# A layer of state-space mixer, cross-attention and 32 experts on one core: two experts' tokens gathered together, and a front in another order

## The chip, the cores and the metric

The kernel is one program on one core of a Trainium2 chip, all in float32. The metric is device time in microseconds; the kernel before has 1097.64 us as the median of three runs (1095.42 to 1098.23). The core's engines are TensorE (PE, with its weight loads shown apart as PEld), VectorE (DVE), ScalarE (ACT), GpSimd (POOL) and SyncE (SP, which here only issues transfers). Data come from HBM through 16 DMA engines into SBUF; TensorE writes its products into eight PSUM banks. A float32 product shows as two MATMUL records in the trace.

## The reference, cut to what matters

256 tokens of 1024 values go through one layer:

```
u, xq = split(x @ w_in, [768])
y_mix = s5(u)                     # 48 groups: y = sum_k C A^k B u, then gelu, then a gated linear unit
y_mem = softmax(xq k^T / 8) v     # k = mem @ mem_w_k, v = mem @ mem_w_v, 4 heads
h     = layer_norm(2**0.25 * x + concat(y_mix, y_mem) @ w_out)
gates, experts = top 4 of softmax(h @ router_w + router_b)
for each expert e of 32:          # its own tokens only
    gu = h[tokens] @ w_gu[e] + b_gu[e]               # 1024 x 2048
    a  = min(gu0, 7) * sigmoid(1.702 * min(gu0, 7)) * (clip(gu1, -7, 7) + 1)
    out[tokens] += gate * (a @ w_down[e] + b_down[e])  # 1024 x 1024
return layer_norm(2**0.25 * h + out)
```

Every expert's weights are read once: 8 MB and 4 MB, 32 times.

## The kernel before, in words

SBUF holds one big tile of 22 slots of 8 KB per partition (1 MB each). The table `slot_of` (L85 to L92) says which names share a slot one after the other, such as "win_2 tz1 gb". The experts' weights stream through a ring (L99) of ten blocks of two slots: one block is 2 MB, an expert takes six of them (four for gate and up, two for down), and a block's transfer is issued by SP, in program order, once the last reader of whatever stood in its two slots is done. All transfers have eight lanes: the ninth waits for the first to land. So the first ten blocks depend on when the front of the kernel lets go of its slots, and the later ones on TensorE's progress in the expert loop.

**The front.** L180 to L228 issue the loads: the rows of the state matrix (`araw`, `ldt`) on ACT's queue, all others on SP's. TensorE turns `araw` into the bank `pp`; VectorE copies it to `par` (L239) and from there computes for the 48 groups the powers of the state matrix, a long chain of small operations, and then the tables `m1p0..2` and `m20..2` (`power`, L468 to L479: two products of 128x2048 and one sum, the second product in a scratch slot `ptmp0` or `ptmp1`; the sum is on GpSimd unless another engine is named). Beside that TensorE transposes x, projects it (`ups`, `qps`), and from `m1p` makes the kernel rows `kb`, which ACT copies to `kr`. VectorE adds the skip weights `dsk` to `kr` (L562), and TensorE turns the result (`kc`, L613 to L619) into the Toeplitz tiles `tz0..2`; these are set to zero first (L546 to L548) and completed by `shifted(b)` (L621), five copies on ACT each. Then come the scores, `m1tp`, `sip`, `stp`, `vmp`, the two passes of `yb` (Toeplitz, L757; with the states `xs`, L818), the softmax's scaling of `prob` by ACT (L736 to L739) and its transposes (`pTp`), the gated linear unit (`zp`), the output projection `yp` (L924 to L945), and the norm.

**The output projection.** Four banks (two token halves i, two column halves hf) sum over eight rows q of `w_out`. The first two are done early (`out_mem`). Of the others, q from 2 to QO - 1 go round the four banks in turn; then each bank in turn gets the rest and is added and measured by VectorE at once. QO is 6. Token half 0 can be normed when its two banks are done.

**The expert loop** (L1252 to L1301). One expert in TensorE's order: `up` (`gu_e`, 64 records, four blocks), the sum of the pair before (`cb_e`, after even experts) or the transposed gates (`ogp_e`, after odd ones), `gather` for the next expert (`xgp_e`: eight column blocks of h times a 128x64 one-hot, two token halves, 32 records), the transposed activations (`atp_e`), the next expert's bias products (`gu_e<-bgu`), and `down` (`dn_e`, 32 records, two blocks). VectorE and ACT do the activation (`act`, L1071) beside it. At expert 22 a block leaves the ring and is used for the rows of the end (`late` with the experts' biases, `rows2` with the last norm's rows); expert 26 transposes the gates and adds the biases (`combine(..., late)`), expert 28 spreads the norm's rows (`spread_gb2`, `bc_e`). The end (`finish`, L1207) norms the sum and writes it.

The order of each queue is pinned to program order in the front (`pin`, L116) for PE, DVE, ACT and SP; GpSimd's and the loop's DVE and ACT instructions are placed by a scheduler.

```
        up(ps, xg, lambda kt: gu[kt], ...)
        ...
            xg = gather_of(e + 1)
            slot_gates_of(e + 1)
        ...
        at = act_t(f"e{e}", a)
        if e + 1 < NE:
            ps = up_bias(f"e{e + 1}", sel_of(e + 1))
        down(f"e{e}", at, ...)
```

## Time and profile before

| what | value |
|---|---|
| median of three runs | 1097.64 us |
| the profiled execution | 1097.22 us, of which 1095.4 us are the span that the profile shows |
| PE busy | 1057.1 us (97%) |
| DVE, ACT, POOL busy | 283.1, 152.6, 44.9 us |
| moved by DMA | 424.69 MB |

The share of busy time is a mean over two very different stages: a front of some 164 us, in which a chain runs through VectorE, ACT and TensorE, and the expert loop, in which TensorE and the DMA engines are both busy almost always. The rows of each stage are therefore read by themselves: the profile's strips by slices and stretches tell what the DMA engines did, the chain of waits tells which of the two ended last, and the timelines tell what the front waited for.

### The profile page before, as it was taken

Reading aid. Unit: us, or ns where it says so; the run is one execution under the profiler, and the core shown is the slowest. Engines: PE = TensorE matmul, PEld = TensorE weight load, DVE = VectorE, ACT = ScalarE, POOL = GpSimd, SP = SyncE. Lnnn points to the kernel's source line nnn. Section 1 sums busy time; section 2 is a strip of 40 time slices with the busy share of each in tenths; the row PEclk is TensorE's granted clock in tenths of the full one; section 3 lists DMA queues with packets and bytes.
Section 4 is the critical chain, followed back from the end, with each engine's and each line's share of the span. In section 5 each row is a group of like instructions: output and inputs, shape, how many; then the busy total and the mean of one; then the engine's idle time right before and its main releaser. Section 6 shows DMA issues by size and latency. Waiting matters only on the chain.

```text
span 1095.4 us, 13424 instructions
## 1 busy us (share of the span) xinstructions
PE 1057.1 (97%) x5781; PEld 503.2 (46%) x5781; DVE 283.1 (26%) x632; ACT 152.6 (14%) x287; POOL 44.9 (4%) x57
## 2 busy tenths in 40 slices
PE   8988999999999999999999999999899999999994
PEld 7875664444444444444444443434343444444331
DVE  6895052121212121212121212111121212121204
ACT  2475111100000000000001010000000000010002
POOL 1700030000000000000000000000000000000001
PEclk9999999999999999999999999999999999999998
DMA  9838968999999999999999999999999999999991
GB/s 301 128 113 284 425 249 346 427 427 426 427 425 428 428 424 428 428 425 427 427 426 427 427 427 427 427 427 425 415 426 427 427 427 428 425 427 427 426 393 56
DMA packets 43813, 424.69 MB, mean 388 GB/s; under 512 B 11311, under 2 KB 14275, under 8 KB 19173
## 3 DMA queue, kind: packets, MB, share of 16 engines
q1 hardware_dynamic: 43268, 423.23, 94.0%
q8 instruction: 47, 0.77, 0.3%
q10 hardware_dynamic: 480, 0.55, 0.1%
q14 instruction: 18, 0.14, 0.0%
HBM read 421.93 MB, written 1.84 MB: 387 GB/s over the span
## 4 chain that ended last, share of the span: by engine, by line
PE 68%; DMA 16%; DVE 1%; ACT 0%; issue 0%; ACTq 0%; POOL 0%; DVEq 0%; SPq 0%
PE gu_e L142 34%; PE dn_e L142 17%; DMA big<-in_exp_w_gu_dram 12%; PE xgp_e L142 9%; PE cb_e L142 5%; DMA big<-in_exp_w_down_dram 4%; PE atp_e L145 1%; DVE big L135 0%; PE accp L142 0%; PE ogp_e L145 0%; PE lgp L142 0%; PE bc_e L142 0%; DVE st L135 0%; PE busy L142 0%; PE hTp L145 0%
## 5 line engine op out<-in xcount | busy, mean ns | idle before, releaser
L142 PE MATMUL gu_e<-big,xg_e 128*64 128x512 f32 x2048 | 448.1, 593 | 12.1 <-DMA big<-in_exp_w_gu_dram 11.2
L142 PEld LDWEIGHTS gu_e<-big,xg_e 128*64 128x64 f32 x2048 | 145.6, 137 | 308.6 <-issue 281.3
L142 PE MATMUL dn_e<-big,xl_te 128*64 128x512 f32 x1024 | 226.8, 595 | 0.7 <-ACT xl_te L135 0.7
L142 PEld LDWEIGHTS dn_e<-big,xl_te 128*64 128x64 f32 x1024 | 70.7, 137 | 154.0 <-issue 127.9
L142 PEld LDWEIGHTS xgp_e<-oh_e,big 128*128 128x128 f32 x1024 | 124.4, 196 | 7.2 <-issue 4.0
L1074 DVE TENSOR_SCALAR xl_e<-gu_e 128x512 f32<-128x512 f32 x32 | 22.1, 692 | 405.9 <-PE gu_e L142 405.9
L142 PE MATMUL xgp_e<-oh_e,big 128*128 128x64 f32 x1024 | 124.4, 280 | 0.0
L1103 DVE COPY y_e<-dn_e 64x512 f32<-64x512 f32 x32 | 21.9, 684 | 257.6 <-PE dn_e L142 257.6
L135 ACT ACTIVATE sg_e<-xl_e 128x512 f32<-128x512 f32 x32 | 20.1, 630 | 383.5 <-DVE xl_e L1074 383.5
L142 PE MATMUL cb_e<-y_e,ogT_e 128*128 128x512 f32 x120 | 55.8, 604 | 0.0
L135 ACT COPY y_e<-dn_e 64x512 f32<-64x512 f32 x32 | 18.6, 582 | 259.1 <-DVE y_e L1103 251.9
L135 ACT COPY xg_e<-xgp_e 128x512 f32<-128x512 f32 x32 | 18.7, 585 | 161.7 <-PE xgp_e L142 161.7
L148 DVE TENSOR_TENSOR big<-big,cb_e 128x512 f32<-128x512 f32 x56 | 36.1, 681 | 6.1 <-PE cb_e L142 6.1
L142 PEld LDWEIGHTS cb_e<-y_e,ogT_e 128*128 128x128 f32 x120 | 21.6, 189 | 32.6 <-issue 29.4
L142 PE MATMUL gu_e<-bgu,ident 32*64 32x512 f32 x256 | 34.8, 612 | 0.0
L135 DVE TENSOR_TENSOR big<-big 128x768 f32<-128x768 f32 (+10 forms) x37 | 27.9, 763 | 15.4 <-ACT big L135 14.3
L151 DVE TENSOR_SCALAR oh_e<-iota,rk 128x64 f32<-128x64 f32 x62 | 12.9, 252 | 71.3 <-PE xgp_e L142 71.3
L142 PE MATMUL yp<-big 128*128 128x512 f32 x64 | 28.2, 595 | 0.0
L135 DVE TENSOR_TENSOR big<-big,tab 128x2048 f32<-128x2048 f32 x12 | 26.6, 2280 | 3.5 <-POOL big L148 3.3
L148 POOL TENSOR_TENSOR big<-big 128x512 f32<-128x512 f32 (+1 forms) x10 | 26.0, 2617 | 14.6 <-DVE big L135 13.8
L1182 POOL MEMSET big<- 128x1280 f32 (+1 forms) x2 | 2.1, 1058 | 576.1 <-PE gu_e L142 576.1
L1076 DVE TENSOR_SCALAR xr_e<-gu_e 128x512 f32<-128x512 f32 x32 | 22.1, 692 | 3.1 <-PE gu_e L142 0.2
(260 smaller groups left out, 567.1 us busy)
## 6 DMA issues: line engine op xcount, KB each, us to landing
big<-in_exp_w_gu_dram SPq DMA_DIRECT2D x128, 2048.0 KB, 31.1
big<-in_exp_w_down_dram SPq DMA_DIRECT2D x63, 2048.0 KB, 32.2
big<-in_l_w_in_dram SPq DMA_DIRECT2D x8, 512.0 KB, 8.5
big<-in_w_out_dram SPq DMA_DIRECT2D x3, 1024.0 KB, 8.1
big<-in_x_dram SPq DMA_DIRECT2D x4, 512.0 KB
big<-in_l_s_w_glu_dram SPq DMA_DIRECT2D x2, 768.0 KB
big<-in_mem_dram SPq DMA_DIRECT2D x1, 1024.0 KB
big<-in_mem_w_k_dram SPq DMA_DIRECT2D x1, 1024.0 KB
```

What stands on the lines that cost most here:

```text
L135: return lambda *a, **k: pin(f(*a, **k))
L142: pin(PE.matmul(o, lhsT, rhs, start=start, stop=stop, skip_group_check=shared))
L145: pin(PE.transpose(o, in_, ident if idn is None else idn))
L148: return (eng or V).tensor_tensor(out=o, in0=x0, in1=x1, op=op)
L151: return (eng or V).tensor_scalar(out=o, in0=x0, scalar1=s1, scalar2=s2, op0=op0, op1=op1)
L1074: V.tensor_scalar(out=xl_, in0=ps[0], scalar1=7.0, scalar2=None, op0=ALU.min)
L1076: V.tensor_scalar(out=xr, in0=ps[1], scalar1=7.0, scalar2=-7.0, op0=ALU.min, op1=ALU.max)
L1103: eng(y[:, 512 * dh : 512 * dh + 512], ps[dh][64 * dh : 64 * dh + 64, :])
L1182: G.memset(t[:, 0:width], 0.0)
```

## The change

It has four parts.

1. **The loop.** `gather` takes a list of ranks: after an odd expert it gathers the tokens of the next two at once (a 128x128 one-hot, two banks), and after an even one nothing. The first two experts are still gathered singly. The sigmoid is written over the bank of its input (`sg = ps[0]`) instead of a tile of SBUF. 
2. **The rows of the end.** A block leaves the ring at expert 18 instead of 22, the biases are added at expert 20 instead of 26, the norm's rows are spread at expert 24 instead of 28.
3. **The first loads.** `araw` goes first on SP's queue, one half of x on ACT's; `w_in` comes in 5 transfers instead of 8, with the state's input rows between them; `dsk` in one instead of four.
4. **The order of the front's sums.** The sum of `m1p2` goes from GpSimd to VectorE, that of `m21` from VectorE to GpSimd; the zeroing of `tz0` and `tz1` goes ahead of the sums of `m20` and `m21`; `shifted(2)` goes ahead of the second half of `vmp`; QO is 4. For the earlier zeroing, `tz0..2`, `wo3` and `wgl0` change slots, and the ring's order follows.

```diff
-        "ptmp0 wsc", "ptmp1 gt", "m20", "m21", "m22", "u_sb", "cab s_in tw yg", "memT xs", "bbt wo3", "bab att",
...
+        "ptmp0 wsc", "ptmp1 gt", "m20", "m21", "m22", "u_sb", "cab s_in tw yg", "memT xs", "bbt tz0", "bab att",
...
-    ring = [2 * k + n for k in (0, 1, 2, 3, 4, 5, 6, 7, 9, 8) for n in range(0, 2, ROWS)]
+    ring = [2 * k + n for k in (0, 1, 2, 3, 4, 6, 8, 7, 9, 5) for n in range(0, 2, ROWS)]
...
+    SP.dma_start(araw[:, 0, :], a_re)
     S.dma_start(ldt, log_dt.rearrange("(g o) -> g o", o=1))
-    S.dma_start(araw[:, 0, :], a_re)
-    S.dma_start(araw[:, 1, :], a_im)
-    for i in range(2):
-        SP.dma_start(x_sb[:, i, :], x[0, i * P : (i + 1) * P, :])
+    SP.dma_start(araw[:, 1, :], a_im)
+    S.dma_start(x_sb[:, 0, :], x[0, 0:P, :])
+    SP.dma_start(x_sb[:, 1, :], x[0, P : 2 * P, :])
...
-        for k in range(2):
-            kt = 2 * k2 + k
-            SP.dma_start(t[:, k, :], w_in[kt * P : (kt + 1) * P, :])
-            win.append(t[:, k, :])
-        if k2 == 0:
-            for raw, re, im in ((rawb, b_re, b_im), (rawc, c_re, c_im)):
-                SP.dma_start(raw[:, 0], re)
-                SP.dma_start(raw[:, 1], im)
+        rows = w_in[2 * k2 * P : (2 * k2 + 2) * P, :].rearrange("(k p) n -> p k n", p=P)
+        for k in (slice(0, 1), slice(1, 2)) if k2 == 0 else (slice(0, 2),):
+            SP.dma_start(t[:, k], rows[:, k])
+        win += [t[:, 0, :], t[:, 1, :]]
+        if k2 < 2:
+            raw, re, im = ((rawb, b_re, b_im), (rawc, c_re, c_im))[k2]
+            SP.dma_start(raw[:, 0], re)
+            SP.dma_start(raw[:, 1], im)
...
-    for j in range(4):
-        SP.dma_start(
-            dsk[32 * j : 32 * j + 32].rearrange("p g h -> p (g h)"),
-            d_skip[192 * j : 192 * j + 192].partition_broadcast(32),
-        )
+    SP.dma_start(
+        dsk.rearrange("p g h -> p (g h)"),
+        bass.AP(tensor=d_skip.tensor, offset=d_skip.offset, ap=[[192, 4], [0, 32], [1, 192]]),
+    )
...
-    def power(name, j, k0, m, eng=G):
...
-        tt(o, o, ptmp[j % 2], ALU.add, eng)
+        if eng is not None:
+            tt(o, o, ptmp[pt], ALU.add, eng)
         return o
...
-    m1p_t = [power(f"m1p{j}", j, 0, (bba, bbb)) for j in range(3)]
+    m1p_t = [power(f"m1p{j}", j, 0, (bba, bbb), j % 2, (G, G, V)[j]) for j in range(3)]
...
-    dbg("@M2", None)
-    m2 = [power("m20", 0, 1, (ca, cb)), power("m21", 1, 1, (ca, cb), V)]
...
+    tz = [big_tile(f"tz{b}") for b in range(3)]
+    kr = big_tile("kr")[:, 0 : 12 * 144].rearrange("p (b n) -> p b n", b=12)
+    for b in range(2):
+        G.memset(tz[b], 0.0)
+    m2 = [power("m20", 0, 1, (ca, cb), 0), power("m21", 1, 1, (ca, cb), 1, None)]
...
-    tz = [big_tile(f"tz{b}") for b in range(3)]
-    for t in tz:
-        G.memset(t, 0.0)
-    kr_t = big_tile("kr")
-    kr = kr_t[:, 0 : 12 * 144].rearrange("p (b n) -> p b n", b=12)
     G.memset(kr[:, :, 0:NH], 0.0)
+    G.memset(tz[2], 0.0)
+    tt(m2[1], m2[1], ptmp[1], ALU.add, G)
...
-    m2 = groups(m2 + [power("m22", 2, 1, (ca, cb), V)])
+    m2 = groups(m2 + [power("m22", 2, 1, (ca, cb), 0, V)])
...
     proj("vmp", vm, lambda q, kt: memT[:, kt, P * q : P * q + P], lambda q, kt: wv[:, kt, :], (0,))
+    shifted(2)
...
     rotated(g_re, s_re, s_im, ALU.add)
-    shifted(2)
...
-    QO = 6
+    QO = 4
...
-    def gather(n, rank, base, between=lambda: None):
-
-        oh = wt((P, 2, CAP), "oh", n)
-        ps = bank(f"xgp_{n}")
+    def gather(n, xg, ranks, base, between=lambda: None):
+
+        w = CAP * len(ranks)
+        oh = wt((P, 2, 2 * CAP), "oh", n)
+        ps = [bank(f"xgp{k}_{n}") for k in range(len(ranks))]
         for i in range(2):
             if i:
                 between()
-            ts(oh[:, i, :], base, rank[i], ALU.is_equal)
+            for k, rank in enumerate(ranks):
+                ts(oh[:, i, CAP * k : CAP * k + CAP], base, rank[i], ALU.is_equal)
             for kt in range(KT):
+                c = w * kt % 512
                 mm(
-                    ps[:, CAP * kt : CAP * kt + CAP], hv[:, i, kt // ROWS, kt % ROWS], oh[:, i, :],
-                    kt == 0 and i == 0, i == 1, True,
+                    ps[w * kt // 512][:, c : c + w], hv[:, i, kt // ROWS, kt % ROWS], oh[:, i, 0:w],
+                    c == 0 and i == 0, i == 1, True,
                 )
-        xg = wt((P, KT, CAP), "xg", n)
-        S.copy(xg, ps.rearrange("p (k c) -> p k c", k=KT))
-        return xg
+        k = 512 // w
+        for n_, p in enumerate(ps):
+            S.copy(xg[:, k * n_ : k * n_ + k, :], p.rearrange("p (k c) -> p k c", k=k))
...
-        sg = wt((P, 512), "sg", n)
+        sg = ps[0]
...
-    xg = gather_of(0, rest_of_ranks)
+    xgs = wt((P, KT, 2 * CAP), "xg", "e0")
+    gather("e0", xgs[:, :, 0:CAP], [ranks_of(0)], iota64, rest_of_ranks)
...
-        if e == NE - 10:
+        if e == NE - 14:
...
-        up(ps, xg, lambda kt: gu[kt], lambda kt: preload(1, kt - 5) if e == NE - 1 and kt in (5, 6) else None)
+        up(ps, xgs[:, :, CAP * (e % 2) : CAP * (e % 2) + CAP], lambda kt: gu[kt], lambda kt: preload(1, kt - 5) if e == NE - 1 and kt in (5, 6) else None)
...
-        if e == NE - 6:
+        if e == NE - 12:
             gates_e(late)
-        if e == NE - 4:
+        if e == NE - 8:
...
-            combine(*last, late if e == NE - 6 else None)
+            combine(*last, late if e == NE - 12 else None)
...
         if e + 1 < NE:
             if e % 2:
                 ogT = gates_t(f"e{e}", og, P)
                 og = wt((P, 2, 2 * CAP), "og", f"e{e + 1}")
-            xg = gather_of(e + 1)
-            slot_gates_of(e + 1)
+                xgs = wt((P, KT, 2 * CAP), "xg", f"e{e + 1}")
+                gather(f"e{e + 1}", xgs, [ranks_of(e + 1), ranks_of(e + 2)], iota64)
+                slot_gates_of(e + 1)
+                slot_gates_of(e + 2)
+            elif e == 0:
+                gather("e1", xgs[:, :, CAP : 2 * CAP], [ranks_of(1)], iota64)
+                slot_gates_of(1)
```

**The sums of the front, on VectorE.** The rows from the first product of `m20` (the before) and from the second product of `m1p1` (the after); `tab0` and `tab1` are the powers' tables, a row without a table is a sum, the row with `dsk` is the addition to `kr` for which TensorE's `kc` waits. Before:

```order
L135 TENSOR_TENSOR big_61<-big_61,tab0_421 128x2048
L135 TENSOR_TENSOR big_61<-big_61,tab1_422 128x2048
L135 TENSOR_TENSOR big_61<-big_61,tab0_421 128x2048
L135 TENSOR_TENSOR big_61<-big_61,tab1_422 128x2048
L135 TENSOR_TENSOR big_61<-big_61 128x2048
L135 TENSOR_TENSOR big_61<-big_61,dsk_114 128x12x16
```

The same place with the change, again on VectorE:

```order
L135 TENSOR_TENSOR big_61<-big_61,tab1_416 128x2048
L135 TENSOR_TENSOR big_61<-big_61,tab0_415 128x2048
L135 TENSOR_TENSOR big_61<-big_61,tab1_416 128x2048
L135 TENSOR_TENSOR big_61<-big_61 128x2048
L135 TENSOR_TENSOR big_61<-big_61,tab0_415 128x2048
L135 TENSOR_TENSOR big_61<-big_61,tab1_416 128x2048
L135 TENSOR_TENSOR big_61<-big_61,tab0_415 128x2048
L135 TENSOR_TENSOR big_61<-big_61,tab1_416 128x2048
L135 TENSOR_TENSOR big_61<-big_61,dsk_111 128x12x16
```

Ten products and one sum stand ahead of the addition in both; the sum has moved from the end of the ten (`m21`) to after the sixth (`m1p2`).

**The output projection, on TensorE.** The last rows of `yp` and the first transposes of the router (`hTp`); the four numbers are the banks (two of token half 0, two of half 1). Before:

```order
L142 MATMUL yp_1041<-big 128x512
L142 MATMUL yp_1042<-big 128x512
L142 MATMUL yp_1043<-big 128x512
L142 MATMUL yp_1044<-big 128x512
L142 MATMUL yp_1041<-big 128x512 x2
L142 MATMUL yp_1042<-big 128x512 x2
L142 MATMUL yp_1043<-big 128x512 x2
L142 MATMUL yp_1044<-big 128x512 x2
L145 MATMUL hTp_1300<-ident,big 128x128 x4
```

With the change:

```order
L142 MATMUL yp_1035<-big 128x512
L142 MATMUL yp_1036<-big 128x512
L142 MATMUL yp_1037<-big 128x512
L142 MATMUL yp_1038<-big 128x512
L142 MATMUL yp_1035<-big 128x512 x4
L142 MATMUL yp_1036<-big 128x512 x4
L142 MATMUL yp_1037<-big 128x512 x4
L142 MATMUL yp_1038<-big 128x512 x4
L145 MATMUL hTp_1294<-ident,big 128x128 x4
```

Token half 0 is complete after 16 of the 24 products instead of after 20, and its norm has eight products beside it instead of four.

**The loop, on TensorE.** After expert 1's `up`, from the transposed gates to `down`. Before:

```order
L145 MATMUL ogp_e_1571<-ident,og_e_1415 128x128 x2
L142 MATMUL xgp_e_1578<-oh_e_1577,big 128x64 x16
L145 MATMUL atp_e_1601<-ident,xr_e_1564 128x128 x4
L142 MATMUL gu_e_1608<-bgu,ident 64x512
L142 MATMUL gu_e_1609<-bgu,ident 64x512
```

With the change:

```order
L145 MATMUL ogp_e_1562<-ident,og_e_1409 128x128 x2
L142 MATMUL xgp_e_1570<-oh_e_1569,big 128x128 x4
L142 MATMUL xgp_e_1571<-oh_e_1569,big 128x128 x4
L142 MATMUL xgp_e_1570<-oh_e_1569,big 128x128 x4
L142 MATMUL xgp_e_1571<-oh_e_1569,big 128x128 x4
L145 MATMUL atp_e_1598<-ident,xr_e_1556 128x128 x4
```

The sixteen products that served one expert have become sixteen of twice the width that serve two; after the even expert that follows none stand.

## Rows read from the trace of the kernel before

**Rows 1.** The page's strips in 40 slices: granted clock in tenths, DMA's GB/s.

```profile
PEclk9999999999999999999999999999999999999998
GB/s 301 128 113 284 425 249 346 427 427 426 427 425 428 428 424 428 428 425 427 427 426 427 427 427 427 427 427 425 415 426 427 427 427 428 425 427 427 426 393 56
```

**Rows 2.** Stretches: us, busy of PE, PEld, DVE, ACT, POOL, clock, DMA share, GB/s.

```profile
150.00:155.00 5.00, 3.27 (x21) 2.08 (x18) 3.33 (x9) 1.15 (x2) 4.21 (x4) 0.82 0.54 231
165.00:170.00 5.00, 5.00 (x26) 1.64 (x24) 2.30 (x9) 2.02 (x6) 0.00 (x0) 1.00 0.31 66
770.00:790.00 20.00, 17.36 (x90) 6.36 (x91) 1.55 (x5) 1.67 (x3) 0.00 (x0) 1.00 1.00 414
```

**Rows 3.** The chain that ended last, in the expert loop: start, us, what.

```profile
230.73 3.63 PE cb_e L142 x8
...
260.72 3.72 PE xgp_e L142 x32
...
286.76 3.63 PE cb_e L142 x8
...
691.35 37.74 DMA big<-in_exp_w_gu_dram
```

**Rows 4.** Timeline of PE at the start: start, us, instruction, idle before it.

```profile
1.13 4.21 PE L142 MATMUL busy<-ones 128*128 128x128 f32 x18 [1.13 <-DVE ones L135]
...
7.40 0.37 PE L145 MATMUL pp<-ident,araw 48*64 48x48 f32 x2 [0.80 <-DMA araw<-in_l_s_a_im_dram]
```

**Rows 5.** Timeline of DVE in the front.

```profile
7.80 0.30 DVE L135 COPY par<-pp 64x144 f32<-64x144 f32 x1 [3.11 <-PE pp L145]
...
28.34 15.47 DVE L135 TENSOR_TENSOR big<-big,tab 128x2048 f32<-128x2048 f32 x7 [0.19 <-DMA gl<-in_ln_g_dram]
...
47.12 6.68 DVE L135 TENSOR_TENSOR big<-big,tab 128x2048 f32<-128x2048 f32 x3 [3.31 <-POOL big L148]
...
53.84 3.38 DVE L135 TENSOR_TENSOR big<-big 128x2048 f32<-128x2048 f32 x1
...
57.14 0.35 DVE L135 TENSOR_TENSOR big<-big,dsk 128x192 f32<-128x192 f32 x1
...
87.94 7.48 DVE L135 TENSOR_TENSOR big<-big 128x744 f32<-128x744 f32 x8
```

**Rows 6.** Timeline of PE in the front.

```profile
57.54 4.50 PE L145 MATMUL kc<-ident,big 128*128 128x128 f32 x24 [3.94 <-DVE big L135]
...
89.31 1.08 PE L142 MATMUL yb<-big 128*32 128x128 f32 x32 [1.72 <-ACT big L135]
...
95.99 2.83 PE L142 MATMUL yb<-big 128*32 128x128 f32 x96
...
125.22 20.87 PE L142 MATMUL yp<-big 128*128 128x512 f32 x48
...
152.17 1.22 PE L145 MATMUL hTp<-ident,big 128*128 128x128 f32 x8 [1.73 <-DVE big L135]
...
164.00 11.38 PE L142 MATMUL gu_e<-big,xg_e 128*64 128x512 f32 x52 [0.67 <-ACT xg_e L135]
```

**Rows 7.** Timeline of ACT: the third `shifted`, and the scaling of `prob`.

```profile
86.13 3.12 ACT L135 COPY big<-big 32x512 f32<-32x512 f32 x5
...
89.28 3.30 ACT L135 ACTIVATE big<-big,sm 128x256 f32<-128x256 f32 x8
```

**Rows 8.** Timeline of SP's queue: the six blocks of expert 1.

```profile
126.30 31.00 SPq L135 DMA_DIRECT2D big<-in_exp_w_gu_dram  x4
167.70 3.76 SPq L135 DMA_DIRECT2D big<-in_exp_w_down_dram  x2
```

**Rows 9.** Timeline of PE at the end of the last expert.

```profile
1064.31 3.65 PE L142 MATMUL gu_e<-big,xg_e 128*64 128x512 f32 x16
...
1071.75 7.09 PE L142 MATMUL dn_e<-big,xl_te 128*64 128x512 f32 x32 [0.72 <-ACT xl_te L135]
```

**Rows 10.** The stretch in which the last transfer lands, columns as in Rows 2.

```profile
1071.00:1072.00 1.00, 0.28 (x3) 0.20 (x4) 0.00 (x0) 0.58 (x1) 0.00 (x0) 1.00 0.03 12
```

More of the change, by code (lines that the diff above doesn't have):

```diff
@@ L466, with power @@
     ptmp = [big_tile(f"ptmp{k}") for k in range(2)]
-    def power(name, j, k0, m, eng=G):
+    def power(name, j, k0, m, pt, eng=G):
         gs = slice(16 * j, 16 * j + 16)
         o = big_tile(name)
-        for dst, mat, tb in ((o, m[0], tab[0]), (ptmp[j % 2], m[1], tab[1])):
+        for dst, mat, tb in ((o, m[0], tab[0]), (ptmp[pt], m[1], tab[1])):
             tt(
@@ L1146, in load_down, with ranks_of @@
         return w
-    def gather_of(e, *between):
-        return gather(f"e{e}", [rk[:, i, e : e + 1] for i in range(2)], iota64, *between)
+    def ranks_of(e):
+        return [rk[:, i, e : e + 1] for i in range(2)]
     def slot_gates_of(e):
@@ L1335 @@
                 erank = [er[:, i : i + 1] for i in range(2)]
-                xg = gather(f"f{rnd}", erank, base)
+                xg = wt((P, KT, 2 * CAP), "xg", f"f{rnd}")[:, :, 0:CAP]
+                gather(f"f{rnd}", xg, [erank], base)
                 slot_gates(og[:, :, 0:CAP], erank, [eg[:, i : i + 1] for i in range(2)], base)
```

1 line of the change is left out of this document (added), and 4 rows, old and new, of the table slot_of.

## The prediction

> **What bounds the kernel now.** I read first the page's strips [rows 1], then stretches of the expert loop [rows 2], then the chain that ended last [rows 3], then the timelines of the front [rows 4 to 8] and of the end [rows 9, 10].
>
> The strips show two stages. In the first seven slices of 27.4 us the DMA rate is uneven; from the eighth to the 38th it is 415 to 428 GB/s throughout [rows 1]. In 770 to 790 us, where TensorE waits for weights, the rate is 414 GB/s at a DMA share of 1.00 [rows 2]: the engines have nothing to add. The chain names TensorE up to 691 us, and DMA after it [rows 3]. That is no contradiction. Two experts cost TensorE 286.76 - 230.73 = 56.0 us, 28.0 us each, while the 12.58 MB of an expert at 427 GB/s take 29.5 us. TensorE starts with blocks that landed during the front, eats 1.5 us of that lead per expert, and has none left at 691 us. Both are full; what can't be compressed is the stream.
>
> The stream has one place where it starts for good. Blocks 7 to 10 are issued between 126.30 and 157.30 us as the front frees their slots; block 11 waits for the first two products' blocks of expert 0 and is issued at about 167.7 us [rows 8]. Just before it the DMA share is 0.31 [rows 2]: all earlier blocks have landed. From there 182 blocks of 2.097 MB, 381.7 MB, take 894 us at 427 GB/s, to some 1064 us in the mean over the engines; the slowest finish at about 1071.2 us [rows 10]. So the time is: the start of `gu_e` of expert 0 (164.00, [rows 6]), a stream of fixed length, and what is left after the last byte. The change can win in the first and the last of these.
>
> **The loop.** An `xgp_e` of 32 records takes 3.72 us [rows 3], 116 ns each. With 128 columns the number of records per pair is 32 instead of 64 and the weights per record are the same. The cost per record lies between 116 ns, if the weights' side bounds it, and 152 ns, the 128-column transposes of the router (1.22 us for 8, part of them at a granted clock of 0.82 [rows 2, 6]); I take 122 ns, near the lower end, since the row at 116 ns has the same weights and full clock. A pair then costs 3.9 us instead of 7.4: 3.5 us less, over 15 pairs some 53 us of TensorE. TensorE needs 26.2 us per expert against the stream's 29.5, so its lead is gone after some eight experts instead of eighteen, and the saving becomes waiting. I put it at nothing but for the end. The cover is the stream: if that ran faster, all 53 us would show. Adding the biases and spreading the norm's rows moves six and four experts forward: the same products, in a stretch where TensorE waits anyway. One block less in the ring from expert 18: before, it is missing from expert 22 on, and the lowest slice, 415 [rows 1], lies where it is taken out: (427 - 415) / 427 x 27.4 = 0.8 us, which now falls in another place and is no new cost. The sigmoid in PSUM adds no instruction; it keeps a bank until the last product of `act`, which TensorE's next step waits for already: 0, between -1 and 1 us in all, since only the last expert's `act` is on the path.
>
> A wait before every block is new in its frequency. In 770 to 790 us TensorE has exactly that, 2.6 us idle in 20, and the granted clock is 1.00; where it idled 1.7 of 5 us it was 0.82 [rows 2]. The Trainium skill, TensorE: Matmul & The Clock Gate, section on HAM oscillation, says that products shorter than the wait for the next transfer let the clock fall back before each step. By that rule a block's products would run at half clock; by the row they do not, and the sum keeps full clock. No run here shows 26.2 us of work in 29.5.
>
> **The first loads.** The first `pp` products wait for `araw`, the last until 7.40 us, and `par` is copied at 7.80 [rows 4, 5]. With `araw` first on SP its rows land sooner; then the warming products, which end at 1.13 + 4.21 = 5.34, are the bound: the `pp` products, 0.63 us in all, and `par` at about 6.1, 1.7 us earlier. x now stands behind `araw` by two issues, and `xT` starts behind the warming products that follow `pp` anyway. Bounds: 0 (x or `ldt` is as late) and 2.1 us (7.40 - 5.34). The other merged transfers are waited for by nobody in this stage: 0.
>
> **The sums.** VectorE waits 3.31 us for GpSimd's sum of `m1p2`, which still reads the scratch slot, ahead of the last three products [rows 5]. With the sum on VectorE the wait goes; the number of sums ahead of the addition to `kr` stays one. From 28.34 - 1.7 = 26.6: ten products of 15.47 / 7 = 2.21 us, one sum at 3.38 (as long as the one removed, GpSimd working beside both), the addition 0.35 and gaps: 52.6 us. TensorE has been idle 3.94 us before `kc` at 57.54 [rows 6], so it was ready at 53.6, and with its own earlier start (about 1.5 us) at 52. `kc` then starts at 52.6: 4.9 us earlier, the 1.7 included. What is late next is TensorE itself, 0.6 us behind. GpSimd gets the zeroing in front and `m21`'s sum behind it; `m2` is read only at 95.99 [rows 6], 35 us later. Bounds for both parts together: 3.3 (no gain from the loads) and 5.5 us (TensorE alone).
>
> **`shifted(2)`.** The third bank of `yb` waits 1.72 us for it [rows 6]; on ACT it runs from 86.13 for 3.12 us, and the scaling of `prob` waits behind it [rows 7]. Ahead of the second half of `vmp` it fills ACT's wait, so the transposes of `prob` come some 2.4 us sooner. But the second pass of `yb` (95.99) also needs `xs`, which VectorE finishes at 87.94 + 7.48 = 95.42 [rows 5], and that moves by 4.9 only, to 90.5. The second pass starts at 90.6: 5.4 earlier. VectorE is late next.
>
> **QO.** The 24 products take 20.87 us [rows 6], 0.87 each. Half 0 is complete at 139.1 instead of 142.6, so its norm and GpSimd's four products after it lie beside the last eight products, and half 1 is normed before TensorE has done with half 0's router. The wait of 1.73 us before `hTp` goes [rows 6]. The clock of 0.82 in this stretch [rows 2] rests on that idle time; the router's products after it can gain up to another 1.3 us. I take 2.7, between 1.7 and 3.1. `wo1` is read later, so block 8 is issued some 6 us later; but blocks 8 to 10 have landed long before block 11 can start, as the 0.31 shows: 0.
>
> Front: 5.4 + 2.7 = 8.1 us.
>
> **The end.** TensorE runs without a wait through the last six experts now, and `down` ends at 1071.75 + 7.09 = 1078.8, 7.6 us after the last byte. With TensorE waiting for the stream, the last block of `up` lands two blocks, 9.8 us, ahead of the last byte. After it come 3.65 us of products, 3.8 us of activation (1067.96 to 1071.75), and 7.1 of `down` [rows 9]: 14.5 - 9.8 = 4.7 us after the last byte. 2.9 us less; bounds 0 (landings as uneven as the end of the transfers) and 6 us (the last block is early).
>
> Sum: 8.1 + 2.9 = 11.0 us. The profiled execution took 1097.22 us, 1.8 more than its span and 0.4 less than the median of the runs: 1086.2 to 1086.6. I forecast **1086.4**.
>
> **The rivals.**
> *The gather counts in full.* If TensorE bounds the loop, as the chain up to 691 us says, 53 us more go: about 1033. Against it: the stretch from 691 us on with waits for DMA, at an unchanged rate.
> *The front's gain does not reach the stream.* If something else than expert 0's start releases block 11, such as the lanes or a slot freed later in the new ring, only the end's 2.9 us remain: 1094.7. For it: the ring's order is new and block 8 is later. Against: the 0.31 of DMA share before block 11.
> *Slower, through the clock.* TensorE has 29.5 - 26.2 = 3.3 us of slack per expert. A block's products at the 1.2 GHz level cost 3.65 us more [rows 9]. One such block per expert exceeds the slack by 0.35 us, 11 us over 31 experts, and eats the gain; that is the point from which it decides. With three blocks in two experts it is 1.5 x 3.65 - 3.3 = 2.2 us each: 67 us, about 1153; with one and a bit, 1100 to 1110. For it: 0.82 at 150 us. Against: 1.00 at 770 us. [...]
>
> **How the numbers follow.** Forecast case 0.80, its own range 1081 to 1092 from the bounds of the terms (front 5 to 9, end 0 to 6). Gather in full 0.03, front lost 0.10, clock 0.07. The range 1079 to 1093 leaves out the two far cases and part of the second. 0.3% of 1097.6, about what a measurement can tell from no change, is 3.3 us. Faster: 0.80 + 0.03 and 0.03 of the second, 0.86; same: the rest of the second, 0.07; slower: 0.07.
>
> **What would show it.** `kc` without its 3.94 us of wait, near 52.6; the second `yb` near 90.6; no wait before the second `hTp`; `gu_e` of expert 0 near 156. In the loop, the chain turns to DMA near 370 us instead of 691, waits of about 1.3 us before most blocks of `gu_e`, the rate still 427, the clock at 1.00; the last byte near 1063 and `down` ending some 5 us after it. I am wrong if the rate is no longer 427 while TensorE waits, if the clock falls in the loop, or if block 11 is issued at 167 us as before.

## The result, and the profile after

The changed kernel takes 1085.6 us (median of four runs, 1084.11 to 1086.48) against 1097.3 us beside it (1095.42 to 1098.23): ratio 0.9894, 95% interval 0.9875 to 0.9913, 11.7 us less. The forecast was 1086.4 us. The profiled execution took 1084.11 us (span 1082.4) and is the lowest of the four, so what its trace shows is up to 1.5 us better than the median.

The strips of the page after, with clock and DMA rate, answer to [rows 1]:

```profile
PEclk9999999999999999999999999999999999999998
GB/s 300 169 166 348 302 299 426 427 428 426 427 426 428 426 426 426 428 426 427 425 428 426 430 409 427 426 426 427 426 426 426 427 428 427 426 427 427 427 406 66
```

The stream now starts one slice earlier and runs at the same rate (425 to 430 GB/s, but for one slice). The dent, 409, lies where the block now leaves the ring (expert 18). The stretches of [rows 2] after, and a stretch that holds nearly the whole loop (columns as there):

```profile
150.00:155.00 5.00, 4.33 (x28) 2.75 (x29) 0.74 (x4) 2.73 (x7) 0.00 (x0) 1.00 0.80 331
165.00:170.00 5.00, 5.00 (x40) 3.55 (x36) 2.79 (x5) 0.60 (x1) 0.00 (x0) 1.00 0.99 419
770.00:790.00 20.00, 17.52 (x72) 5.66 (x69) 4.50 (x8) 1.18 (x2) 0.00 (x0) 1.00 1.01 428
160.00:1040.00 880.00, 826.05 (x4018) 316.79 (x4016) 163.73 (x337) 79.91 (x144) 2.05 (x2) 1.00 1.01 426
```

TensorE is idle for 54 of these 880 us, at a granted clock of 1.00 and a rate of 426 GB/s. The chain that ended last (start, us, what) turns to DMA at 343 us instead of 691 [rows 3]:

```profile
245.84 3.77 PE xgp_e L142 x32
...
310.35 13.73 PE gu_e L142 x64
...
343.12 34.59 DMA big<-in_exp_w_down_dram
```

A gather for two experts takes 3.77 us, 118 ns per record. The front on TensorE, answering to [rows 4, 6]:

```profile
5.28 0.40 PE L145 MATMUL pp<-ident,araw 48*64 48x48 f32 x3
...
51.39 2.84 PE L145 MATMUL kc<-ident,big 128*128 128x128 f32 x24 [2.63 <-DVE big L135]
...
77.83 2.83 PE L142 MATMUL yb<-big 128*32 128x128 f32 x96
...
87.65 0.42 PE L142 MATMUL yb<-big 128*32 128x128 f32 x8 [1.84 <-DVE big L135]
88.52 2.61 PE L142 MATMUL yb<-big 128*32 128x128 f32 x88 [0.45 <-DVE big L135]
...
117.53 20.87 PE L142 MATMUL yp<-big 128*128 128x512 f32 x48
...
142.69 1.09 PE L145 MATMUL hTp<-ident,big 128*128 128x128 f32 x8
...
152.87 13.96 PE L142 MATMUL gu_e<-big,xg_e 128*64 128x512 f32 x64 [0.67 <-ACT xg_e L135]
```

From `kc` on, each row stands 6 to 11 us earlier than its partner. The waits of 1.7 us ahead of the third bank of `yb` and the second `hTp` are gone, and `kc` itself is 1.7 us shorter (2.84 instead of 4.50). VectorE, answering to [rows 5], and SP's queue, answering to [rows 8]:

```profile
5.71 0.30 DVE L135 COPY par<-pp 64x144 f32<-64x144 f32 x1 [2.87 <-PE pp L145]
...
26.26 13.28 DVE L135 TENSOR_TENSOR big<-big,tab 128x2048 f32<-128x2048 f32 x6 [0.19 <-DVE big L135]
39.57 2.54 DVE L135 TENSOR_TENSOR big<-big 128x2048 f32<-128x2048 f32 x1
42.04 8.87 DVE L135 TENSOR_TENSOR big<-big,tab 128x2048 f32<-128x2048 f32 x4
50.83 0.51 DVE L135 TENSOR_TENSOR big<-big,dsk 128x192 f32<-128x192 f32 x1
...
80.98 7.48 DVE L135 TENSOR_TENSOR big<-big 128x744 f32<-128x744 f32 x8
```

```profile
118.98 28.02 SPq L135 DMA_DIRECT2D big<-in_exp_w_gu_dram  x4
156.56 3.76 SPq L135 DMA_DIRECT2D big<-in_exp_w_down_dram  x2
```

VectorE goes from the first product to the addition without a stop, and block 11 is issued at 156.6 us instead of 167.7. The end on TensorE, answering to [rows 9]:

```profile
1044.56 1.94 PE L142 MATMUL gu_e<-big,xg_e 128*64 128x512 f32 x8 [1.25 <-DMA big<-in_exp_w_gu_dram]
...
1050.40 3.65 PE L142 MATMUL gu_e<-big,xg_e 128*64 128x512 f32 x16
...
1057.84 7.09 PE L142 MATMUL dn_e<-big,xl_te 128*64 128x512 f32 x32 [0.72 <-ACT xl_te L135]
```

`down` starts 1057.84 - 152.87 = 904.97 us after expert 0's `gu_e`; before it was 1071.75 - 164.00 = 907.75 [rows 6, 9]. From there to the end of the span it is 24.56 us, before 23.65; this difference comes up again in experiment 5.

### The profile page after: what moved, and what is told of

The parts are those of the page before. It is cut to its first block, busy times and chain, and to the rows that moved or that the text cites. A ratio compares the mean times of both kernels' runs of the same rounds, so it can differ in the third digit from the quotient of the medians.

```text
span 1082.4 us, 12437 instructions
## 1 busy us (share of the span) xinstructions
PE 1003.6 (93%) x5301; PEld 437.9 (40%) x5301; DVE 280.1 (26%) x632; ACT 152.8 (14%) x287; POOL 45.2 (4%) x57
## 3 DMA queue, kind: packets, MB, share of 16 engines
HBM read 421.93 MB, written 1.84 MB: 392 GB/s over the span
## 4 chain that ended last, share of the span: by engine, by line
DMA 50%; PE 40%; DVE 8%; issue 1%; ACT 0%; ACTq 0%; POOL 0%; DVEq 0%; SPq 0%
DMA big<-in_exp_w_gu_dram 43%; PE gu_e L142 17%; PE dn_e L142 10%; DMA big<-in_exp_w_down_dram 7%; DVE big L135 5%; PE xgp_e L142 4%; PE yp L142 3%; PE cb_e L142 2%; PE zp L142 1%; PE atp_e L145 1%; PE busy L142 1%; PE lgp L142 0%; PE accp L142 0%; PE bc_e L142 0%; PE ogp_e L145 0%
## 5 line engine op out<-in xcount | busy, mean ns | idle before, releaser
L142 PE MATMUL gu_e<-big,xg_e 128*64 128x512 f32 x2048 | 457.8, 596 | 55.9 <-DMA big<-in_exp_w_gu_dram 55.2
L142 PEld LDWEIGHTS gu_e<-big,xg_e 128*64 128x64 f32 x2048 | 141.3, 137 | 366.3 <-issue 256.4
L135 ACT ACTIVATE gu_e<-xl_e 128x512 f32<-128x512 f32 x32 | 19.2, 601 | 432.3 <-DVE xl_e L1078 432.3
L142 PE MATMUL xgp_e<-oh_e,big 128*128 128x128 f32 (+1 forms) x544 | 67.1, 282 | 0.0
L142 PEld LDWEIGHTS xgp_e<-oh_e,big 128*128 128x128 f32 x544 | 65.5, 197 | 0.1
L142 PEld LDWEIGHTS cb_e<-y_e,ogT_e 128*128 128x128 f32 x120 | 21.7, 190 | 32.5 <-issue 26.1
L135 ACT COPY xl_te<-atp_e 128x512 f32<-128x512 f32 x32 | 18.7, 585 | 56.9 <-PE atp_e L145 50.2
L135 DVE TENSOR_TENSOR big<-big,tab 128x2048 f32<-128x2048 f32 x12 | 26.6, 2278 | 0.2 <-DVE big L135 0.2
L148 POOL TENSOR_TENSOR big<-big 128x512 f32<-128x512 f32 (+1 forms) x10 | 26.1, 2628 | 2.8 <-DVE big L135 1.9
L1081 DVE SCALAR_TENSOR_TENSOR xr_e<-xr_e,xl_e 128x512 f32<-128x512 f32 x32 | 22.0, 689 | 0.5
```

The lines of the kernel that those rows point to most:

```text
L135: return lambda *a, **k: pin(f(*a, **k))
L142: pin(PE.matmul(o, lhsT, rhs, start=start, stop=stop, skip_group_check=shared))
L148: return (eng or V).tensor_tensor(out=o, in0=x0, in1=x1, op=op)
L1081: V.scalar_tensor_tensor(out=xr, in0=xr, scalar=1.0, in1=xl_, op0=ALU.add, op1=ALU.mult)
```

## The experiments

The theory: the time is the start of expert 0, a stream of fixed length, and the end; TensorE's saving in the loop is hidden. Rivals: the gather counts; parts of the front count otherwise than worked out; the clock. Twelve kernels ran, each timed beside the kernel before (1097.0 to 1097.3 us); "start" is the start of expert 0's `gu_e`, "stretch" the time from there to `down` of the last expert (904.97 in the changed kernel), "tail" the time from there to the end of the span (24.56). The changed kernel's four runs spread over 2.4 us, so a difference of medians under some 2 us is told only where the traces show where it lies.

**1. The front of the kernel before, the loop of the changed one.** The edit puts back the slots, the ring, the loads, the sums, `shifted(2)` and QO; in the changed kernel's terms:

```diff
-    QO = 4
+    QO = 6
...
-    m1p_t = [power(f"m1p{j}", j, 0, (bba, bbb), j % 2, (G, G, V)[j]) for j in range(3)]
+    m1p_t = [power(f"m1p{j}", j, 0, (bba, bbb), j % 2, G) for j in range(3)]
...
```

> The changed kernel with the whole front of the kernel before: slots and ring, first loads, sums, shifted(2), QO = 6. What is left of the change is the gather in pairs, the sigmoid in PSUM and the earlier rows of the end. Theory (the gain is the start of the stream, the loop's saving is hidden): gu_e of expert 0 starts at 164 us again, the last byte lands near 1071, down ends some 6 us after it instead of 7.6, so about 1.5 to 2 us are left of the gain: 1095.5 us. Rival (the gain is the gather's, 53 us of TensorE that count in part): 1086, no worse than the whole change.

Measured: 1094.61 us, ratio 0.9977 (0.9967 to 0.9987). Start 163.92, stretch 904.92. The loop, the rows of the end and the sigmoid together are worth 2.6 us, all of it in the stretch; the front is worth the other 9.0. The slots, the ring's order and the sigmoid were not tried by themselves. The rival falls.

**2. Single gather, all else changed.**

```diff
-                gather(f"e{e + 1}", xgs, [ranks_of(e + 1), ranks_of(e + 2)], iota64)
...
+            c = CAP * ((e + 1) % 2)
+            gather(f"e{e + 1}", xgs[:, :, c : c + CAP], [ranks_of(e + 1)], iota64)
...
```

> The changed kernel, but each expert's tokens are gathered by products of their own (64 columns), as before; front and end stay changed. Theory: TensorE needs 28.0 us per expert again, under the stream's 29.5; it leads until some 680 us, the stream is as long as before; only the end's 1.5 to 2 us are lost: 1087.3 us. Rival (the gather makes the gain): near 1097.

Measured: 1088.87 us, ratio 0.9925 (0.9911 to 0.9938). The chain turns to DMA at 603.54 us, and the stretch is 908.44: 3.5 us longer, more than the 1.5 to 2 expected and near the prediction's 2.9. TensorE's 53 us are worth 3.3 us. Without the pair gather the other edits of the loop gain nothing: the stretch is 0.7 us longer than before (907.75), and why is open.

**3. QO = 6 again.**

```diff
-    QO = 4
+    QO = 6
```

> The changed kernel with QO = 6, the order of the products of yp as before. Theory: half 0 is complete four products later, hTp waits again, gu_e of expert 0 starts 2.7 (prediction) to 3.4 us (difference of the two traces) later, and all of it reaches the end: 1088.3 to 1089.0 us. Rival (the stage after yp runs faster for another reason, such as slots or the earlier transfers): 1085.6.

Measured: 1090.37 us, ratio 0.9937 (0.9923 to 0.995): 4.8 us at the medians. In its trace `yp` starts 0.56 us later than in the changed kernel, and the way from there to the start takes 38.84 us instead of 35.34: 3.5 us is what QO does in this execution, the fastest of the five; the rest of the 4.8 has no trace. The wait is back, and the router's products behind it are slower. Here, and then in the changed kernel:

```profile
145.04 1.18 PE L145 MATMUL hTp<-ident,big 128*128 128x128 f32 x8 [1.73 <-DVE big L135]
...
146.51 3.53 PE L142 MATMUL lgp<-y_hT,wg 128*32 128x128 f32 x16
```

```profile
144.04 1.93 PE L142 MATMUL lgp<-y_hT,wg 128*32 128x128 f32 x16
```

**4. The sums put back.**

```diff
-    m1p_t = [power(f"m1p{j}", j, 0, (bba, bbb), j % 2, (G, G, V)[j]) for j in range(3)]
+    m1p_t = [power(f"m1p{j}", j, 0, (bba, bbb), j % 2, G) for j in range(3)]
...
-    m2 = [power("m20", 0, 1, (ca, cb), 0), power("m21", 1, 1, (ca, cb), 1, None)]
+    m2 = [power("m20", 0, 1, (ca, cb), 0), power("m21", 1, 1, (ca, cb), 1, V)]
```

> The changed kernel with the sums and the zeroing as before: m1p2 summed on GpSimd, m21 on VectorE before kc. Theory: VectorE waits 3.3 us for GpSimd again, kc starts 3.2 (prediction) to 4.0 us (difference of the traces less the first loads) later, and so does the second pass of yb, since VectorE bounds it: 1088.8 to 1089.6 us. Rival (TensorE or ACT is the bound between kc and yb, and takes most of it): 1086 to 1087.

Measured: 1091.17 us, ratio 0.9946 (0.9933 to 0.996): 5.6 us, more than either expected. VectorE, then TensorE, in its trace:

```profile
46.99 6.68 DVE L135 TENSOR_TENSOR big<-big,tab 128x2048 f32<-128x2048 f32 x3 [4.95 <-POOL big L148]
```

```profile
57.42 4.31 PE L145 MATMUL kc<-ident,big 128*128 128x128 f32 x24 [3.95 <-DVE big L135]
```

VectorE waits 1.6 us longer than before for GpSimd, and `kc` starts where it started in the kernel before (57.54): without the new sums the earlier loads are worth nothing to it. GpSimd, ahead of the sum of `m1p2`, works on `dsk` (which lands at 31.1 us here) and then zeroes a tile (40.69 to 42.46 us), so that its sum ends at 46.9 us, as before (47.0). So what this experiment takes away is the sums and, at `kc`, the loads' gain as well. And `kc` takes 4.31 us instead of 2.84. That led to experiment 9.

**5. The first loads put back.**

```diff
-    SP.dma_start(araw[:, 0, :], a_re)
     S.dma_start(ldt, log_dt.rearrange("(g o) -> g o", o=1))
-    SP.dma_start(araw[:, 1, :], a_im)
+    S.dma_start(araw[:, 0, :], a_re)
+    S.dma_start(araw[:, 1, :], a_im)
...
```

> The changed kernel with the first loads as before (ldt and araw on ACT's queue, x on SP's, w_in in eight transfers, d_skip in four), the sums in the new order. Theory: VectorE's seven products start 2.1 us later (28.3 instead of 26.3), kc too. TensorE then waits 4.7 us before kc instead of 2.6, and in the kernel before a wait of 3.9 us was followed by kc at a granted clock of 0.60 to 0.83 (4.50 us instead of 2.84). So 2.0 us if the clock holds, 3.6 us if it falls: 1087.6 to 1089.3. Rival (as with the sums put back, where the earlier loads moved kc by 0.1 us only, the loads are worth nothing): 1085.6.

Measured: 1085.85 us (1085.77 to 1087.06), ratio 0.9899 (0.9884 to 0.9914): no difference that can be told. `kc` starts 2.5 us later, with a wait of only 2.00, since TensorE is later too. In this profiled execution, its slowest run, the start is 4.0 us later; the second pass of `yb` took longer:

```profile
90.16 0.43 PE L142 MATMUL yb<-big 128*32 128x128 f32 x8 [1.84 <-DVE big L135]
91.03 4.10 PE L142 MATMUL yb<-big 128*32 128x128 f32 x88 [0.44 <-DVE big L135]
```

The same waits, 1.84 and 0.44 us, stand ahead of it in the changed kernel, where it took 2.61. In 85 to 95 us the granted clock is 0.83 here and 1.00 there. Experiment 2, whose front is the changed kernel's, has a clock of 0.83 and 4.28 us there too. So there is a place where the clock falls in some executions and holds in others, and 1.5 to 1.7 us depend on it.

The earlier loads also cost something at the other end. The tail is 23.69 us here and 24.56 in the changed kernel. It is 24.5 to 24.8 us in all nine kernels with the new first loads, and 23.65 to 23.69 in all five without (the kernel before, experiments 1, 5, 9 and 11). The difference lies behind the last copy on ACT, where only the output is under way: from there to the end of the span it is 3.25 us here and 4.15 in the changed kernel. The output's transfers on ACT's queue (KB each, us from issue to landing) here, and in the changed kernel:

```profile
out_dram<-big ACTq DMA_DIRECT2D x2, 256.0 KB, 2.1
```

```profile
out_dram<-big ACTq DMA_DIRECT2D x2, 256.0 KB, 2.6
```

So the new first loads cost some 0.9 us behind the last instruction. How they do that, no run shows.

**6. `shifted(2)` put back.**

```diff
     proj("vmp", vm, lambda q, kt: memT[:, kt, P * q : P * q + P], lambda q, kt: wv[:, kt, :], (0,))
-    shifted(2)
...
     rotated(g_re, s_re, s_im, ALU.add)
+    shifted(2)
```

> The changed kernel with shifted(2) in its old place on ACT, behind the scan. Theory: the third bank of yb waits 1.7 us for ACT again, but the second pass of yb waits for xs on VectorE, which does not move; only the transposes of prob come later, and TensorE's wait before the second pass of yb (1.8 + 0.45 us) shrinks: 0 to 0.5 us lost, 1085.6 to 1086.1. Rival (ACT is the bound there, the wait of 1.7 us and the 2.4 us behind it count): 1087.3 to 1088.

Measured: 1085.61 us, ratio 0.9899 (0.9883 to 0.9914). The second pass of `yb` starts at 88.11, with no wait; the start is 152.79. The wait for ACT has only changed places with the one for VectorE.

**7. More work on TensorE, less than the slack.**

```diff
+        if 0 < e < NE - 1:
+            busy(8)
         down(f"e{e}", at, lambda kk: dn[kk], y[64 * (e % 2) : 64 * (e % 2) + 64, :])
```

> The changed kernel with 8 more products of 128x128 on TensorE ahead of down of experts 1 to 30, whose results nobody reads: 8 x 236 ns = 1.9 us per expert, 57 us in all, about what the pair gather saves. Theory: TensorE needs 26.1 + 1.9 = 28.0 us per expert, less than the stream's 29.5; the loop's length does not change, the end loses up to 2 to 3 us as with the gather of one expert: 1085.6 to 1088.5. Rival (TensorE's work counts in full): 1142.

Measured: 1086.47 us, ratio 0.9905 (0.989 to 0.992). Stretch 906.96, 2.0 us longer. Its waits for DMA, and those of the changed kernel (sum of us, times, longest):

```profile
PE gu_e L142 <- DMA big<-in_exp_w_gu_dram: 8.1, 10, 1.3
```

```profile
PE gu_e L142 <- DMA big<-in_exp_w_gu_dram: 55.2, 51, 1.6
```

57 us of work took the place of 47 us of waits, and the time rose by 0.9 us at the medians.

**8. More than the slack.** As 7, with `busy(16)`.

> The same with 16 products: 3.8 us per expert, 113 us in all. TensorE then needs 29.9 us per expert, more than the stream's 29.5, and bounds the loop. In the changed kernel TensorE waits 71 us in all between expert 0 and the end (span 1082.4 less 152.9, less 31 x 26.1, less 49 for the last expert and the finish). Theory (what is beyond the slack shows, and no more): 113 - 71 = 42 us more, about 1128. Rival (slack of 3.3 us per expert as the prediction worked it out from the two rates): 30 x 0.5 = 15 us more, about 1101. Rival (in full): 1199.

Measured: 1130.09 us, ratio 1.0305 (1.0291 to 1.0319): 44.5 us more, against 42. TensorE is busy without a gap, and the rate falls:

```profile
400.00:695.00 295.00, 295.00 (x1594) 138.09 (x1592) 53.22 (x110) 25.03 (x45) 2.05 (x2) 1.00 1.00 415
695.00:990.00 295.00, 295.00 (x1580) 138.93 (x1578) 53.06 (x109) 26.94 (x49) 0.00 (x0) 1.00 0.99 412
```

This is the picture of a loop bound by TensorE. The slack is what the trace leaves between the start and the end, 71 us by the expectation's sum (55 of them show as waits for DMA), not 3.3 us for each expert: it takes TensorE seven experts (152.9 to 343 us) to eat its lead. The trace also shows what the earlier loads can cost; TensorE's second part of `ups`, and VectorE's first product behind it:

```profile
17.56 8.41 PE L142 MATMUL ups<-big 128*128 128x256 f32 x24 [1.20 <-DMA big<-in_l_w_in_dram]
```

```profile
28.06 2.29 DVE L135 TENSOR_TENSOR big<-big,tab 128x2048 f32<-128x2048 f32 x1 [1.98 <-DMA gl<-in_ln_g_dram]
```

In the changed kernel's profiled execution the same products took 5.45 us without a wait. Here TensorE comes ahead of `w_in`, waits, runs the products at a granted clock of 0.65 (18 to 26 us), and VectorE starts at 28.06 instead of 26.26. What ended VectorE's wait is inferred; that `cabp`, which frees the slot it writes to, ended only 0.1 us before, is in the trace. TensorE waits 0.3 to 1.2 us for `w_in` at this place in seven of the nine traces with the new first loads, but in the other eight VectorE starts at 26.1 to 26.6 us; only here it is late.

**9. The kernel before with unread products in two of its waits.**

```diff
             ps = bank(f"kc{b}{a}")
+            for _ in range(0 if b or a else 13):
+                mm(ps[:, 0:P], ones, ones, True, True)
...
             ps = bank(f"hTp{i}{k4}")
+            for _ in range(6 if (i, k4) == (1, 0) else 0):
+                mm(ps[:, 0:P], ones, ones, True, True)
```

> The kernel before, with 13 products whose results nobody reads in TensorE's wait of 3.94 us ahead of kc (3.1 us of work) and 6 in its wait of 1.73 us ahead of the second hTp (1.4 us). Nothing else is changed, and the waits' ends stay where they are. Theory (a part of the front's gain is the granted clock after these waits: kc took 4.50 us at 0.60 to 0.83 and 2.84 at 1.00; the router's products 3.23 and 1.93): 1.7 + 1.3 = 3.0 us less, 1094.2 us, kc at 2.84 us and the clock at 1.00 in both stretches. Rival (the clock there has another reason, or the next wait takes the gain back): 1097.2.

Measured: twelve runs in two groups, seven from 1094.27 to 1094.91 us and five from 1098.84 to 1099.73; ratio over all 0.9999 (0.9986 to 1.0012). The profiled execution is of the lower group. The stretch after `kc`'s start in the kernel before, and then here:

```profile
57.00:60.00 3.00, 2.46 (x12) 2.46 (x13) 3.00 (x4) 0.74 (x2) 0.01 (x1) 0.60 0.45 178
60.00:63.00 3.00, 3.00 (x20) 2.87 (x19) 2.97 (x2) 2.01 (x5) 0.00 (x0) 0.83 0.01 3
```

```profile
57.00:60.00 3.00, 2.71 (x25) 2.71 (x26) 3.00 (x3) 1.72 (x5) 0.00 (x0) 1.00 0.77 308
60.00:63.00 3.00, 3.00 (x17) 2.64 (x16) 2.96 (x2) 2.92 (x6) 0.00 (x0) 1.00 0.01 4
```

```profile
57.29 2.84 PE L145 MATMUL kc<-ident,big 128*128 128x128 f32 x24 [1.05 <-DVE big L135]
...
151.81 1.93 PE L142 MATMUL lgp<-y_hT,wg 128*32 128x128 f32 x16
```

The router's products in the kernel before:

```profile
153.88 3.23 PE L142 MATMUL lgp<-y_hT,wg 128*32 128x128 f32 x16
```

`kc` takes 2.84 us instead of 4.50, the router's products 1.93 instead of 3.23, and the start is 161.32, 2.7 us earlier, with nothing changed but TensorE's idle time. In the lower group the gain is there; on the mean over the twelve it is not. The five runs, 4.4 us longer, have a lower granted clock over the whole span (0.988 to 0.992) than the seven (0.993 to 0.996), so the clock seems to fall somewhere in them; where, and why, has no trace and stays open.

**10. Guards.** Unread products ahead of `babp` (5) and of the second pass of `yb` (7), and two additions moved:

```diff
...
-lambda kt: preload(1, kt - 5) if e == NE - 1 and kt in (5, 6) else None
+lambda kt: preload(1, kt // 2 - 1) if e == NE - 1 and kt in (2, 4) else None
...
```

> The changed kernel with three small edits: 5 such products ahead of babp (so that a late transfer of w_in finds TensorE at work), 7 in the wait of 1.84 us ahead of the second pass of yb, and the last expert's first two additions of acc moved from the third and fourth blocks of gu (kt 5, 6) to the second and third (kt 2, 4), where TensorE waits for DMA. The runs of the changed kernel lie between 1084.1 and 1086.5 us; in the traces at hand the second pass of yb takes 2.61 us in some and 4.1 to 4.3 in others, and VectorE's first product starts at 26.1 to 26.6 in most and at 28.1 in one where TensorE waited for w_in. Theory (these two are the spread): every run near the lowest, less 0.9 us at the end: 1083.2 us, with down starting 904.1 us after gu_e of expert 0 instead of 905.0. Rival (the spread comes from the stream): 1085.6.

Measured: 1084.31 us (1083.43 to 1085.37), ratio 0.9887 (0.9872 to 0.9901): 1.3 us under the changed kernel's median, inside the intervals, so not shown to be better. The spread is 1.9 us instead of 2.4: the guards do not remove it. The second pass of `yb` took 2.61 us at a clock of 1.00, but in this execution VectorE's sum of `m1p2` took 4.02 us instead of 2.54, so `kc` started at 52.90. The reason is on GpSimd, which here waits longer for the merged `dsk` before its own two sums. GpSimd in the changed kernel, then GpSimd and VectorE's sum here:

```profile
30.14 0.59 POOL L148 TENSOR_TENSOR dsk<-dsk,same 128x192 f32<-128x192 f32 x1 [12.37 <-DMA dsk<-in_l_s_d_dram]
30.88 9.08 POOL L148 TENSOR_TENSOR big<-big 128x2048 f32<-128x2048 f32 x2
```

```profile
31.84 0.59 POOL L148 TENSOR_TENSOR dsk<-dsk,same 128x192 f32<-128x192 f32 x1 [14.02 <-DMA dsk<-in_l_s_d_dram]
32.39 9.07 POOL L148 TENSOR_TENSOR big<-big 128x2048 f32<-128x2048 f32 x2
```

```profile
39.60 4.02 DVE L135 TENSOR_TENSOR big<-big 128x2048 f32<-128x2048 f32 x1
```

GpSimd's sums end at 39.96 us there and at 41.46 here, and VectorE's sum ends some 2.15 us after that in both (42.11 and 43.62). In every trace of this case VectorE's sum ahead of `kc` ends 2.14 to 2.16 us after the GpSimd sum beside it. So the spread has a third source, which the expectation lacked: when `dsk` lands. The stretch is 904.49, 0.5 us less instead of 0.9.

**11. Guards, and the first loads put back.** The edits of 5 and 10 together.

> The same with the first loads as before. Theory (the first loads are worth 2.0 us once the clock ahead of the second pass of yb no longer differs between runs; that put back by themselves they cost only 0.3 us at the median was the spread): 1085.2 us, kc 2.0 to 2.5 us later. Rival (the first loads are worth nothing): 1083.2.

Measured: 1084.78 us (1084.64 to 1085.72), ratio 0.9896 (0.9882 to 0.9911). 0.5 us more than 10: less than the expected 2.0, and not told from nothing. `kc` starts at 53.85, only 0.95 later than in 10, whose sum of `m1p2` was the long one (4.02 us against 3.11 here), and the tail is 23.65 us against 24.83. Stretch 903.93.

**12. Half of the middle products of `gu` left out.**

```diff
...
-                for hf in range(2):
+                for hf in range(1 if some and kt not in (0, KT - 1) else 2):
...
```

> The changed kernel where experts 1 to 30 leave out half of the products of gu for the six middle rows kt 1 to 6 (their result is not the layer's). TensorE then needs 26.1 - 5.5 = 20.6 us per expert and waits 2 to 3 us before each block of gu, with 1.8 to 2.7 us of products behind each wait. Theory (the stream alone sets the loop, the waits are harmless): 1085.6 us, clock 1.00 in the loop. Rival (waits longer than the products behind them let the clock fall): about 0.5 to 0.8 of granted clock in the loop; the time stays within some 3 us as long as products at 1.2 GHz still fit into the stream's 29.5 us, and is over 1100 us if they do not (20.6 x 2 = 41 us).

Measured: 1085.02 us, ratio 0.9901 (0.9886 to 0.9915), clock 1.00 in the loop. But the experiment did not do what it should: a block takes as long with half of its records. A middle block here, and the same one in the changed kernel:

```profile
421.94 3.65 PE L142 MATMUL gu_e<-big,xg_e 128*64 128x512 f32 x8 [0.27 <-DMA big<-in_exp_w_gu_dram]
```

```profile
421.88 3.65 PE L142 MATMUL gu_e<-big,xg_e 128*64 128x512 f32 x16 [0.18 <-DMA big<-in_exp_w_gu_dram]
```

So it says nothing on longer waits; what it shows instead stands in the last section.

## Why the prediction was right, step by step

**The bound** was right. The rate stayed at 425 to 430 GB/s but for the slice at the dent, block 11 moved with expert 0, and experiments 2, 7 and 8 show TensorE's work hidden up to 71 us and showing beyond. The gather's 3.9 us per pair measured 3.77, TensorE's 26.2 us per expert 26.1 ((310.18 - 257.94) / 2, two starts of `gu_e` a pair apart). The chain turns to DMA at 343 us, 27 us earlier than forecast; the waits are there, 51 of 1.1 us in the mean, so ahead of about half of the blocks from there on, not of most. (One slip that nothing rests on: the stream from 167.7 us for 894 us ends at 1061.7 in the mean, not at 1064.) With that the rival "gather in full" falls by experiments 1 and 2, and "front lost" by experiment 1.

**The clock rival** did not come: 1.00 throughout the loop, as the row at 770 us said. The rule of the Trainium skill that the prediction weighed (TensorE: Matmul & The Clock Gate, HAM oscillation) speaks of products shorter than the wait; here 3.65 us of products stand behind waits of at most 1.6 us, so the traces do not contradict it, they lie outside it. By its own forecast of waits of 1.3 us the prediction should have seen that: the rule did not say that a block's products would run at half clock. What the prediction overlooked is that the clock was at work in its front, in the other direction, ahead of `kc`.

**The front** was forecast at 8.1 us. At the medians it is worth 9.0 (experiment 1 against the changed kernel). Since 0.9 us of its gain are lost again in the tail (experiment 5), it brings expert 0 some 9.9 us forward; in the traces 11.1, of which up to 1.5 is that the profiled run is the lowest.
- *The sums and the first loads* can't be split cleanly, since experiment 4 took away the loads' gain at `kc` too (5.6 us in all). Together they were to bring `kc` 4.9 us forward; in the profiled execution it is 6.15. Of that, 2.1 us are the first product's earlier start instead of 1.7, and 3.3 the wait that is gone, as forecast. The step that failed is the size of the sum, 3.38 us "as long as the one removed": that one had 1.2 us of a GpSimd sum beside it, the new one 0.4, and took 2.54 us. A second step failed with it: only the start of `kc` was moved, and its duration was kept. The wait of 3.94 us had cost the clock as well; with 2.63 us the clock holds and `kc` is 1.7 us shorter (experiment 9 shows it without the sums). Some 0.65 of these 1.7 us reach `xs`: VectorE's wait for TensorE ahead of its scans, shown here in the kernel before, is gone in the changed kernel and in experiment 9, and is there again (0.57) in experiment 4, where `kc` is long.

```profile
78.59 2.88 DVE L135 TENSOR_TENSOR big<-big 128x768 f32<-128x768 f32 x3 [0.65 <-PE stp L145]
```

- *The first loads* by themselves were sized too large: 1.7 us forecast, 0.3 and 0.5 us at the medians (experiments 5 and 11), inside the bounds of 0 to 2.1. VectorE's first product is 2.1 us earlier, the upper bound. But "the other merged transfers are waited for by nobody in this stage: 0" failed. GpSimd waits for the merged `dsk`, and the longest of these waits delays `kc` by 1.5 us (experiment 10). In one of nine traces an earlier TensorE runs into `w_in` and gives 1.8 us back (experiment 8). And a cost stood in no term: some 0.9 us in the tail, in all nine.
- *`shifted(2)`* was given 0.5 us beyond the sums, and is worth 0.0 (experiment 6); that VectorE's `xs` would be late next was right. The second pass of `yb` began 2.1 us earlier than forecast (88.5 against 90.6), with VectorE, not ACT, still last.
- *QO* was forecast at 2.7 us and is worth 3.5 in the trace (experiment 3): 1.73 us of wait and 1.6 + 0.1 us of products that now run at full clock. The row was read and the price seen ("up to another 1.3 us"), but taken only in part; it came in full.

**The end** was forecast at 2.9 us; 2.8 by the stretches before and after, 2.6 by experiment 1. The way there was a little different: the last block of `up` does not wait for the stream, as the additions of `acc` between its products (2.2 us) are later than the landing. With them out of the way (experiments 10 and 11) the stretch is 0.5 and 1.0 us shorter. From `down` on nothing was edited, and still the tail is 0.9 us longer than before; it goes with the first loads, as experiment 5 shows. So the profiled execution shows 13.0 us of span (11.1 + 2.8 - 0.9), not 13.9.

So the sum of 11.0 against 11.7 us is right partly by luck. At the start of expert 0 the forecast was 1.8 us too small (8.1 against 9.9, at the medians), the end was nearly right (2.9 against 2.6), and 0.9 us that no term had were lost in the tail. Within the front, too little for the sums and for QO stood against too much for the loads and for `shifted(2)`.

## What to carry to other kernels

Where a stream of fixed length bounds a loop, saved engine work is worth only what it moves at the two ends: look for the instruction that starts the stream and for what is left after its last byte, and count the slack over the whole loop, lead included, before you add or remove work. A wait on TensorE is worth more than its own length if the rows behind it show a granted clock under 1.00: add the difference of those rows' durations at the two clocks to the price of the wait. Where an engine comes earlier, name the next transfer it can run into, and look at more than one execution before a term under 2 us is believed. When the size of an instruction is taken from another place of the trace, see which engine worked beside it there. And compare the end of the span too, also where nothing was edited.
